# Row maxima and norm scratch in PSUM, operand tiles cleared once, two splits moved to VectorE, in a hybrid decoder layer

## The chip, the core and the metric

The kernel runs on one core of a Trainium2 chip. A core has TensorE for matrix products (PE; its weight loads, which overlap them, are PEld), VectorE (DVE), ScalarE (ACT), GpSimd (POOL), and SyncE (SP), which issues most of the DMAs. Operands lie in SBUF, products are summed in PSUM banks of 128 partitions x 2 KB. The metric is the device time of one execution in microseconds, the median of several runs.

## What is computed

One layer of a decoder on x of 1 x 1024 x 1024 float32. Three token mixers share one input projection: a Mamba-2 state-space mixer (SSD), stick-breaking attention, and native sparse attention (NSA). They are gated, summed and projected. A conv gated MLP with 2816 hidden channels follows; both halves have a norm before and after. The parts of the reference that the change is in, the norm and the selected (`ss`) and window (`sw`) branches of the sparse attention, whose softmax needs the row maxima:

```python
def rms_norm(x, w):
    xf = x.astype(jnp.float32)
    y = xf * lax.rsqrt(jnp.mean(xf * xf, axis=-1, keepdims=True) + NORM_EPS)
    return (y * w.astype(jnp.float32)).astype(x.dtype)

def masked_softmax(s, mask):
    p = jax.nn.softmax(jnp.where(mask, s, NEG), axis=-1)
    return jnp.where(mask, p, 0.0)
...
        ss = (jnp.einsum('bqghd,bgqnkd->bghqnk', qb, ks).astype(jnp.float32) * scale
              - slopes[None, :, :, None, None, None] * dist_s[:, :, None].astype(jnp.float32))
...
        p_sel = masked_softmax(ss, (dist_s >= 0).reshape(bsz, g, 1, NSA_QBLK, n_sel * SEL_BLOCK))
        o_sel = jnp.einsum('bghqm,bgqmd->bqghd', p_sel.astype(vs.dtype),
                           vs.reshape(bsz, g, NSA_QBLK, n_sel * SEL_BLOCK, dh))
...
        sw = (jnp.einsum('bqghd,bkgd->bghqk', qb, kwb).astype(jnp.float32) * scale
              - slopes[:, :, None, None] * dist_w.astype(jnp.float32))
        o_win = jnp.einsum('bghqk,bkgd->bqghd', masked_softmax(sw, wmask).astype(vwb.dtype), vwb)
```

## The kernel before

Work runs feature-major in tiles of 128 x 512. Products are made in a split form: an operand a is written as hi + lo, where hi is a rounded by a copy on ScalarE to a short float32 form, and lo is the rest, a subtraction on DVE or POOL. A product is then three matmuls, hi by hi, hi by lo and lo by hi. So for every weight tile `whi` comes from ACT (L286, L532) and `wlo` from POOL (L291, L533), and many activations have such a pair too. The tile scheduler decides from a modelled timeline which instruction stands where on each engine. In the NSA stage alone PE's instructions are kept in the order of the program (`in_order`).

**The start.** `first_half` reads x, squares it on ACT and adds the squares on DVE (L430, `ss`). `norm` sums `ss` over the partitions by four small products with ones and calls `rsqrt_mean`, which makes the factor 1/sqrt(mean + eps): a logarithm and an exponential on ACT, and one step of refinement on DVE, L254, L256, L257 and L258, with a scratch tile `rv` and the result `rt`, both 128 x 4 in SBUF. ACT spreads `rt` to `rb` (L451), and PE transposes it. There are two calls at the start (two halves of the tokens) and two at the end, in `norm_rows`.

**The NSA stage** (some 420 to 810 us) has 16 steps of 128 queries for one of two groups of heads. For each step `compressed` builds the query operands Q1 and Q2 and does the compressed branch and the top-k choice; `maxima` finds the row maxima of the scores; `attend` makes scores (`ps_s`), exponentials (`wT`), their split (L996 on ACT, L997 on POOL) and the values. The three run interleaved, and PE follows the interleaving as written. `maxima` takes 8 or more banks `ps_t` in turn (two buffers): each is filled by a product and reduced by DVE into `mx` (L959, the tile having been set by POOL, L942). At the end L962 reduces `mx` to `m`, POOL clears the operand tile `MM` (L964), and DVE writes -m, split in two bfloat16 parts, into four columns of it (L966, L967). After `MM_LAG` = 3 further turns of the interleaving PE transposes MM into a bank, and L973 casts that into rows 96 to 128 of Q1. The score products read Q1.

**The MLP** multiplies blocks of weights and activations by a scheme of seven products in place of eight (`weights7`, `product`), so that sums of blocks (`uf`, `uhi`, `ulo`, L532 to L547) are made of each weight, and sums of activations. L1681 and L1682 split the last of these activation sums: for q = 5 on DVE, for q = 4 on POOL, four tiles k = 0 to 3 each. Product 4 (`ahi`, `alo` by these) is among the first that PE does in a weight group, in a bank `psn`; `ahi` has one buffer. Convolutions (L324 on ACT, L328 and L330 on DVE) follow the products.

Of the kernel before, what the change touches and what calls it, by code (L numbers as in the profile page):

```python
# [10 lines left out]
F32 = mybir.dt.float32  # L11
R32 = mybir.dt.float32r
BF = mybir.dt.bfloat16
AF = mybir.ActivationFunctionType
OP = mybir.AluOpType
# [5 lines left out]
DM = 1024  # L21
# [189 lines left out]
def trunk(ctx: ExitStack, tc: tile.TileContext, A: dict, outT: bass.AP, dbg=None):  # L211
    nc = tc.nc
    act = nc.scalar.activation
    V, P = nc.vector, nc.gpsimd
# [35 lines left out]

    def rsqrt_mean(r, v, ps, n):

        act(r, ps, AF.Ln, scale=1.0 / n, bias=eps)
        V.tensor_scalar(v, ps, 1.0 / n, EPS, op0=OP.mult, op1=OP.add)  # L254
        act(r, r, AF.Exp, scale=-0.5)
        V.tensor_tensor(v, v, r, op=OP.mult)  # L256
        V.scalar_tensor_tensor(v, v, -0.5, r, op0=OP.mult, op1=OP.mult)  # L257
        V.scalar_tensor_tensor(r, v, 1.5, r, op0=OP.add, op1=OP.mult)  # L258
# [115 lines left out]
    n1p = n1.enter_context(tc.tile_pool(name="n1", side="right", reuse_waits="tile", bufs=1))  # L374
# [33 lines left out]
    for h in range(2):  # L408
        for k in range(8):
            x = x_t(F32)  # L410
# [31 lines left out]
    def norm(h, ss):  # L442

        ps = ps_d()
        for n in range(4):
            mm(ps[:, n:n + 1], ss[:, n * 128:(n + 1) * 128], ones[:, 0:1], start=True, stop=True)
        rt, v, rq = [n1p.tile([128, 4], F32, name=f"r{n}", bufs=2) for n in "tvq"]
        rsqrt_mean(rt, v, ps[:, 0:4], DM)
        V.tensor_scalar(rq, rt, 0.125, None, op0=OP.mult)
        rb = n1p.tile([128, 4, 128], F32, name="rb")  # L450
        act(rb, rt[:, :, None].to_broadcast([128, 4, 128]), AF.Copy)  # L451
        r = ps_b()
        for n in range(4):
            tr(r[:, n * 128:(n + 1) * 128], rb[:, n, :], ident)
        return rq, r
# [13 lines left out]
    for h, tiles in ((0, [[ps_s, ps_s, ps_t, ps_t]]), (1, [[ps_o, ps_d], [ps_s, ps_s]])):  # L469
        *pss, ss = first_half(h, tiles)  # L470
        rq, r = norm(h, ss)
# [231 lines left out]
def nsa_stage(nc, tc, es, env):  # L703
    E = L(env)
    A, act, V, P, mm, tr, fl = E.A, E.act, E.V, E.P, E.mm, E.tr, E.fl
# [150 lines left out]

    wk = es.enter_context(tc.tile_pool(name="nsa_q", reuse_waits="tile", bufs=2))

    def compressed(g, i):
        qs = wk.tile([128, 256], F32, name="q_in", bufs=3)  # L860
        nc.sync.dma_start(qs, q_d[g, i])
# [9 lines left out]
        ps = pq[:, 256:]  # L871
# [65 lines left out]
    def maxima(g, i):  # L937
# [5 lines left out]
        for h in range(4):  # L943
            for a in range(2):
# [3 lines left out]
                for n, (c0, c1) in enumerate(parts):  # L948
# [9 lines left out]
                        mm(pm[:, w - 128:w], ident_b, mask_d, start=False, stop=True)  # L958
                    V.tensor_reduce(mx[:, h, a, n:n + 1], pm[:, :w], axis=AX, op=OP.max)  # L959
                    yield  # L960
        m = wk.tile([128, 4, 2], F32, name="m")
        V.tensor_reduce(m, mx, axis=AX, op=OP.max)  # L962
        MM = wk.tile([128, 4, 32], BF, name="MM")
        P.memset(MM, 0.0)  # L964
        mv = MM[:, :, 0:4].rearrange("p h (a s) -> p h a s", a=2)
        V.tensor_scalar(mv[:, :, :, 0], m, -1.0, None, op0=OP.mult)  # L966
        V.scalar_tensor_tensor(mv[:, :, :, 1], m, -1.0, mv[:, :, :, 0], op0=OP.mult, op1=OP.subtract)  # L967
        for _ in range(MM_LAG):
            yield
        p3 = ps_tb()  # L970
        for h in range(4):
            tr(p3[96:128, h * 128:(h + 1) * 128], MM[:, h, :], ident_b)
        V.tensor_copy(Q1[96:128, :], p3[96:128])  # L973
# [82 lines left out]
    for n in range(-2, 17):  # L1056
# [3 lines left out]
        if 0 <= n < 16:  # L1060
            g, i = order[n]
# [316 lines left out]
def tail_stage(nc, tc, es, env):  # L1378
# [300 lines left out]
    for q, k, t, place in sorted(parts, key=lambda x: (-x[0], x[1])):  # L1679
        rhs[q][k] = hi, lo = place(), x_t()  # L1680
        act(hi, t, AF.Copy)  # L1681
        (P if q == 4 else V).tensor_tensor(lo, t, fl(hi), op=OP.subtract)  # L1682

    acc = []

# [117 lines left out]
    def norm_rows(ss, W):  # L1803

        n = W // 128
        ps, r = [psn.tile([128, 512], F32, name="psn", tag="psn") for _ in range(2)]
        for m in range(n):
            mm(ps[:, m:m + 1], ss[:, m * 128:(m + 1) * 128], E.ones[:, 0:1], start=True, stop=True)
        rt, v = [fw.tile([128, 4], F32, name=f"r{x}", bufs=2) for x in "tv"]
        E.rsqrt_mean(rt[:, :n], v[:, :n], ps[:, :n], DM)  # L1810
        rb = up_.tile([128, 512], F32, name="u1", bufs=U1_BUFS)
        act(rb[:, :W].rearrange("p (n t) -> p n t", t=128), rt[:, :n, None].to_broadcast([128, n, 128]), AF.Copy)
        for m in range(n):
            tr(r[:, m * 128:(m + 1) * 128], rb[:, m * 128:(m + 1) * 128], E.ident)
        return r
# [81 lines left out]
```

## Time and profile before

| what | value |
|---|---|
| median of 3 runs | 2262.1 us (2256.22 to 2265.59) |
| the profiled execution | 2260.92 us |
| its span | 2259.2 us |
| granted TensorE clock, mean | 0.989 |
| busy: PE, DVE, POOL, ACT | 2177.4, 1329.9, 1275.1, 1205.2 us |
| share of PE in the chain that ended last | 76% |

Times in the trace are microseconds from the start of the span. A row of the timeline gives start, duration, engine, line, operation, output and inputs, and in square brackets the idle time of the engine just before it and what ended that. PE's matmuls overlap, so the spacing of their starts is shorter than their durations. [...]

### The profile page before, as it was taken

The page shows a single profiled execution, that of the slowest core. Times are in us where ns is not written, and L with a number is a line of the kernel's source. Part 1 is how long each engine was busy: PE and PEld are TensorE (multiplying, and loading weights), DVE is VectorE, ACT ScalarE, POOL GpSimd, SP SyncE. Part 2 cuts the span into 40 slices and gives each one's busy share as a digit, 9 for nine tenths or more (in the row PEclk, how much of TensorE's full clock was granted, in tenths as well). Part 3 has the DMA queues.
Part 4 walks back from the last instruction along what each step waited for, and adds up shares of the span by engine and source line. Part 5 has one row for each costly group of instructions (what it writes and reads, how often), then busy time and mean ns, then how long its engine had stood idle before and what let it go on. Part 6 is the DMA issues. An engine that isn't in the chain of part 4 may idle for free.

```text
span 2259.2 us, 30196 instructions
## 1 busy us (share of the span) xinstructions
PE 2177.4 (96%) x10589; PEld 1736.2 (77%) x10589; DVE 1329.9 (59%) x2499; ACT 1205.2 (53%) x2240; POOL 1275.1 (56%) x1120
## 2 busy tenths in 40 slices
PE   7999999998998999999999999999989999989997
PEld 7888889866665678888775678888778888868887
DVE  8665544258557516556536662228945767675776
ACT  7544443466756746676755441236645444466544
POOL 3776741246746634333337656558687777765743
PEclk9999999999999999999999999999999999999999
DMA  4233342321221011212362174235332323255433
GB/s 172 83 112 108 111 143 62 97 84 29 55 75 33 10 59 38 66 57 79 110 214 76 62 242 144 85 126 181 122 98 80 117 94 112 98 173 186 140 100 120
DMA packets 120105, 234.65 MB, mean 104 GB/s; under 512 B 28816, under 2 KB 43088, under 8 KB 119952
## 3 DMA queue, kind: packets, MB, share of 16 engines
q1 hardware_dynamic: 117072, 230.13, 31.1%
q10 hardware_dynamic: 2880, 2.59, 0.3%
q8 instruction: 83, 1.36, 0.3%
q14 instruction: 70, 0.57, 0.1%
HBM read 169.10 MB, written 63.57 MB: 103 GB/s over the span
## 4 chain that ended last, share of the span: by engine, by line
PE 76%; DVE 9%; ACT 5%; POOL 3%; issue 3%; DMA 2%; DVEq 0%; SPq 0%; ACTq 0%; POOLq 0%
PE dense L219 52%; PE ps_s L219 7%; PE ps_o L219 6%; PE ps_t L219 5%; PE ps_b L219 3%; PE psn L219 3%; DVE mx L959 1%; DVE u L328 1%; DMA lo<-m_d 1%; POOL wlo L533 1%; POOL alo L547 0%; ACT h_hi L423 0%; ACT wT L986 0%; POOL wlo L291 0%; DVE yacc L1023 0%
## 5 line engine op out<-in xcount | busy, mean ns | idle before, releaser
L291 POOL TENSOR_TENSOR wlo<-wraw,whi 128x256 fp32r<-128x256 f32 x344 | 273.7, 827 | 265.9 <-ACT whi L286 264.8
L219 PE MATMUL dense<-h_hi,whi 128*128 128x512 f32 x656 | 262.7, 401 | 0.0
L219 PE MATMUL dense<-h_hi,wlo 128*128 128x512 f32 x656 | 256.7, 392 | 0.3 <-POOL wlo L533 0.3
L219 PE MATMUL dense<-h_lo,whi 128*128 128x512 f32 x656 | 256.5, 391 | 0.0
L997 POOL TENSOR_TENSOR wT_lo<-wT,wT_hi 128x512 fp32r<-128x512 f32 x132 | 168.4, 1287 | 95.3 <-ACT wT_hi L996 86.3
L219 PE MATMUL dense<-hi,whi 128*128 128x512 f32 x576 | 214.3, 391 | 1.2 <-ACT whi L286 1.2
L219 PE MATMUL dense<-hi,wlo 128*128 128x512 f32 x512 | 200.7, 393 | 0.5 <-POOL wlo L291 0.4
L219 PE MATMUL dense<-x,uhi 128*128 128x512 f32 x600 | 191.6, 392 | 1.2 <-ACT x L605 1.2
L219 PE MATMUL dense<-lo,whi 128*128 128x512 f32 x448 | 176.1, 394 | 0.0
L286 ACT ACTIVATE whi<-wraw 128x1024 fp32r<-128x1024 f32 (+1 forms) x94 | 92.6, 985 | 152.7 <-PE dense L219 125.7
L542 POOL TENSOR_TENSOR ulo<-uf,uhi 128x1024 fp32r<-128x1024 f32 x38 | 91.8, 2417 | 117.7 <-ACT uhi L541 117.7
L219 PEld LDWEIGHTS dense<-h_hi,wlo 128*128 128x128 f32 x656 | 123.1, 188 | 27.1 <-POOL wlo L533 0.7
L219 PEld LDWEIGHTS dense<-h_hi,whi 128*128 128x128 f32 x656 | 123.7, 189 | 23.6
L219 PEld LDWEIGHTS dense<-h_lo,whi 128*128 128x128 f32 x656 | 123.5, 188 | 22.6
L219 PEld LDWEIGHTS dense<-x,uhi 128*128 128x128 f32 x600 | 113.0, 189 | 26.2 <-ACT x L605 2.4
L1201 POOL TENSOR_TENSOR s_lo<-sa,s_hi 128x512 fp32r<-128x512 f32 (+2 forms) x48 | 53.7, 1120 | 139.5 <-ACT s_hi L1200 139.5
L219 PEld LDWEIGHTS dense<-hi,whi 128*128 128x128 f32 x576 | 108.4, 188 | 25.6 <-ACT whi L286 2.1
L959 DVE TENSOR_REDUCE mx<-ps_t 128x1 f32<-128x384 f32 (+3 forms) x192 | 98.6, 520 | 46.5 <-PE ps_t L219 42.8
L328 DVE SCALAR_TENSOR_TENSOR u<-dense,pv,u 128x511 f32<-128x511 f32 (+1 forms) x140 | 103.4, 741 | 36.9 <-ACT u L324 36.8
L545 POOL TENSOR_TENSOR ulo<-uf,uhi 128x1024 fp32r<-128x1024 f32 x38 | 91.8, 2415 | 41.1 <-ACT uhi L544 39.7
L986 ACT ACTIVATE wT<-ps_s 128x512 f32<-128x512 f32 x132 | 78.4, 594 | 68.2 <-PE ps_s L219 63.8
L219 PEld LDWEIGHTS dense<-hi,wlo 128*128 128x128 f32 x512 | 96.3, 188 | 23.7 <-POOL wlo L291 2.0
(550 smaller groups left out, 6141.8 us busy)
## 6 DMA issues: line engine op xcount, KB each, us to landing
wraw<-in_wfm SPq DMA_DIRECT2D x62, 512.0 KB, 3.7
wraw<-in_wup SPq DMA_DIRECT2D x52, 512.0 KB, 3.6
lo<-m_d SPq DMA_DIRECT2D x58, 256.0 KB, 3.2
g_d<-gate_e SPq DMA_DIRECT2D x48, 256.0 KB, 2.0
s_d<-o SPq DMA_DIRECT2D x48, 256.0 KB, 2.0
ge<-g_d SPq DMA_DIRECT2D x24, 512.0 KB, 3.5
m_d<-u SPq DMA_DIRECT2D x44, 256.0 KB, 2.0
row<-s_d SPq DMA_DIRECT2D x16, 512.0 KB, 4.8
```

Source lines behind the costliest of these rows:

```text
L219: i = f(*a, **k)
L286: act(hi, raw, AF.Copy)
L291: (V if tiles else P).tensor_tensor(lo[:, s], raw[:, s], fl(hi[:, s]), op=OP.subtract)
L328: V.scalar_tensor_tensor(o[:, d:], ps[:, :512 - d], taps[d], o[:, d:], op0=OP.mult, op1=OP.add)
L533: P.tensor_tensor(wlo, raws[0], fl(whi), op=OP.subtract)
L542: P.tensor_tensor(l24, f24, fl(h24), op=OP.subtract)
L545: P.tensor_tensor(l31, f31, fl(h31), op=OP.subtract)
L959: V.tensor_reduce(mx[:, h, a, n:n + 1], pm[:, :w], axis=AX, op=OP.max)
L986: act(w.rearrange("p h q -> p (h q)"), pz, AF.Exp)
L997: P.tensor_tensor(lo, wf, fl(hi), op=OP.subtract)
L1201: (P if SB_SLO else V).tensor_tensor(s_lo[:, c0:], a[:, c0:], fl(s_hi[:, c0:]), op=OP.subtract)
```

## The change

Four edits. In `maxima` the bank for the transposes is taken before the last reduction; the transposes, bfloat16, use its columns 0 to 256, and `m` is now columns 256 to 264 of the same bank. The two MM tiles are made and cleared once, by DVE, ahead of the stage, and used in turn; the 16 clearings on POOL go, and the columns that are never written stay zero. The scratch of `rsqrt_mean` is four columns of the bank in which the sums lie, at all its four calls. Of the q = 4 splits two (k = 2, 3) go from POOL to DVE.

```diff
@@ norm
-        rt, v, rq = [n1p.tile([128, 4], F32, name=f"r{n}", bufs=2) for n in "tvq"]
-        rsqrt_mean(rt, v, ps[:, 0:4], DM)
+        rt, rq = [n1p.tile([128, 4], F32, name=f"r{n}", bufs=2) for n in "tq"]
+        rsqrt_mean(rt, ps[:, 4:8], ps[:, 0:4], DM)
@@ ahead of the NSA stage
     wk = es.enter_context(tc.tile_pool(name="nsa_q", reuse_waits="tile", bufs=2))
+
+
+    MMs = [wk.tile([128, 4, 32], BF, name=f"MM{n}", bufs=1) for n in range(2)]
+    for MM in MMs:
+        V.memset(MM, 0.0)
@@ maxima
-        m = wk.tile([128, 4, 2], F32, name="m")
+
+        pz = ps_t()
+        p3 = pz[:, :256].bitcast(BF)
+        m = pz[:, 256:264].rearrange("p (h a) -> p h a", a=2)
         V.tensor_reduce(m, mx, axis=AX, op=OP.max)
-        MM = wk.tile([128, 4, 32], BF, name="MM")
-        P.memset(MM, 0.0)
+        MM = MMs[i % 2]
         mv = MM[:, :, 0:4].rearrange("p h (a s) -> p h a s", a=2)
         V.tensor_scalar(mv[:, :, :, 0], m, -1.0, None, op0=OP.mult)
         V.scalar_tensor_tensor(mv[:, :, :, 1], m, -1.0, mv[:, :, :, 0], op0=OP.mult, op1=OP.subtract)
         for _ in range(MM_LAG):
             yield
-        p3 = ps_tb()
@@ the last activation sums of the MLP
-        (P if q == 4 else V).tensor_tensor(lo, t, fl(hi), op=OP.subtract)
+        (P if q == 4 and k < 2 else V).tensor_tensor(lo, t, fl(hi), op=OP.subtract)
@@ norm_rows
-        rt, v = [fw.tile([128, 4], F32, name=f"r{x}", bufs=2) for x in "tv"]
-        E.rsqrt_mean(rt[:, :n], v[:, :n], ps[:, :n], DM)
+        rt = fw.tile([128, 4], F32, name="rt", bufs=2)
+        E.rsqrt_mean(rt[:, :n], ps[:, 4:4 + n], ps[:, :n], DM)
```

PE has as many instructions as before, DVE four more, POOL eighteen fewer. Lines behind the edits move (L254 to L258 become L255 to L259, L966, L967 and L973 become L974, L975 and L980), L1682 becomes L1689.

DVE's order around the maxima of the fourteenth step, first before and then in the new kernel (`m` was a tile, and now the output of the reduction is the bank `ps_t`; Q is Q1, `ps_s` holds attention sums):

```order
L959 TENSOR_REDUCE mx<-ps_t 128x1 x2
L934 CAST Q_7556<-ps_b 32x512
L962 TENSOR_REDUCE m<-mx 128x8
L966 TENSOR_SCALAR MM<-m 128x4x2
L967 SCALAR_TENSOR_TENSOR MM<-m,MM 128x4x2
L1020 RECIPROCAL ps_s<-ps_s 128x4
L1021 TENSOR_TENSOR of<-ps_s,sg 128x4
```

```order
L965 TENSOR_REDUCE mx<-ps_t 128x1 x2
L940 CAST Q_7519<-ps_b 32x512
L971 TENSOR_REDUCE ps_t<-mx 128x8
L974 TENSOR_SCALAR MM_3845<-ps_t 128x4x2
L975 SCALAR_TENSOR_TENSOR MM_3845<-ps_t,MM_3845 128x4x2
L1027 RECIPROCAL ps_s<-ps_s 128x4
L1028 TENSOR_TENSOR of<-ps_s,sg 128x4
```

The places are the same and the operands differ; PE's order in the stage is unchanged, and POOL's lacks the clearings.

POOL at the first weight groups of the MLP, before and after (L1682 and L1689 are the split of the activation sums; `wlo`, `alo`, `ulo` are low parts of weights and their sums):

```order
L547 TENSOR_TENSOR alo<-wraw,ahi 128x512
L539 TENSOR_TENSOR uf_15952<-uf_15951,wraw 128x512
L1682 TENSOR_TENSOR x<-x,lo 128x512 x2
L533 TENSOR_TENSOR wlo<-wraw,whi 128x1024
L540 TENSOR_TENSOR uf_15952<-uf_15952,wraw 128x512
L1682 TENSOR_TENSOR x<-x,lo 128x512 x2
L542 TENSOR_TENSOR ulo<-uf_15952,uhi 128x1024
L545 TENSOR_TENSOR ulo<-uf_15951,uhi 128x1024
L533 TENSOR_TENSOR wlo<-wraw,whi 128x1024
L547 TENSOR_TENSOR alo<-wraw,ahi 128x512
```

```order
L548 TENSOR_TENSOR alo<-wraw,ahi 128x512
L540 TENSOR_TENSOR uf_15906<-uf_15905,wraw 128x512
L1689 TENSOR_TENSOR x<-x,lo 128x512 x2
L534 TENSOR_TENSOR wlo<-wraw,whi 128x1024
L541 TENSOR_TENSOR uf_15906<-uf_15906,wraw 128x512
L548 TENSOR_TENSOR alo<-wraw,ahi 128x512
L543 TENSOR_TENSOR ulo<-uf_15906,uhi 128x1024
L546 TENSOR_TENSOR ulo<-uf_15905,uhi 128x1024
L534 TENSOR_TENSOR wlo<-wraw,whi 128x1024
```

The second pair of splits is gone from POOL, and `alo` of the next weight group, with its `ahi` on ACT, stands ahead of the two `ulo`. On DVE the two splits come in here (only after; u and dense are convolution results and product banks):

```order
L331 SCALAR_TENSOR_TENSOR u_15807<-psn,pv,u_15807 128x2
L1689 TENSOR_TENSOR x<-x,lo 128x512
L1588 TENSOR_TENSOR u_15766<-dense,u_15807 128x512
L1643 TENSOR_TENSOR dense<-dense,snap 128x512
L1689 TENSOR_TENSOR x<-x,lo 128x512
L327 COPY psn<-dense 128x2
```

They lie before and behind the two operations on PSUM that stood there alone. PE's twelve products of `psn` now stand together; before, two products with `uhi` stood ahead of the last two of the twelve.

In the state-space stage and around the middle of the down projection the scheduler gives all engines another order of the same instructions.

## Rows read from the trace of the kernel before

**Rows 1.** The page, busy table and costliest groups: busy us, mean ns, idle before.
```profile
PE 2177.4 (96%) x10589; PEld 1736.2 (77%) x10589; DVE 1329.9 (59%) x2499; ACT 1205.2 (53%) x2240; POOL 1275.1 (56%) x1120
...
L219 PE MATMUL dense<-hi,whi 128*128 128x512 f32 x576 | 214.3, 391 | 1.2 <-ACT whi L286 1.2
```

**Rows 2.** What PE waited for: us in total, times, longest.
```profile
PE ps_t L219 <- DVE MM L967: 6.5, 8, 1.4
...
PE ps_s L219 <- ACT dec L1288: 5.5, 4, 2.1
...
PE ps_s L219 <- DVE Q L973: 4.6, 4, 1.7
PE psn L219 <- POOL x L1682: 4.5, 3, 3.8
PE dense L219 <- ACT snap L1550: 4.1, 4, 2.3
```

**Rows 3.** Stretches: length, busy by engine, granted clock, DMA; and one PE row.
```profile
32.30:39.70 7.40, 7.35 (x34) 7.26 (x35) 6.91 (x12) 4.39 (x11) 2.59 (x2) 0.50 0.17 54
1220.00:1230.00 10.00, 10.00 (x42) 5.71 (x42) 2.57 (x8) 5.90 (x16) 8.70 (x8) 0.54 0.32 107
1669.60:1674.50 4.90, 4.86 (x11) 3.80 (x12) 0.00 (x0) 2.37 (x3) 4.90 (x3) 0.50 0.27 101
...
1218.82 0.49 PE L219 MATMUL ps_s<-half,sel 16*128 16x512 f32 x1 [1.29 <-ACT dec L1288]
```

**Rows 4.** Line L1698 of the down projection: duration ns min/median/max, by inputs.
```profile
L1698 DVE TENSOR_TENSOR lo<-psn,hi x39: 673/682/692, 2014.0 to 2162.5; 128x512 fp32r<-128x512 f32 x39
L1698 DVE TENSOR_TENSOR lo<-lo,hi x19: 674/693/2427, 1987.9 to 2188.9; 128x512 fp32r<-128x512 f32 x19
```

**Rows 5.** Lines around the maxima: ns min/median/max; then busy us, mean ns, idle.
```profile
L966 DVE TENSOR_SCALAR MM<-m x16: 177/178/1040, 443.4 to 771.2; 128x8 bf16<-128x8 f32 x16
L967 DVE SCALAR_TENSOR_TENSOR MM<-m,MM x16: 160/178/1239, 443.6 to 771.5; 128x8 bf16<-128x8 f32 x16
L1020 DVE RECIPROCAL ps_s<-ps_s x32: 174/192/192, 469.8 to 810.1; 128x4 f32<-128x4 f32 x32
L883 DVE RECIPROCAL m<-m x16: 167/169/179, 424.9 to 736.6; 128x4 f32<-128x4 f32 x16
...
L967 DVE SCALAR_TENSOR_TENSOR MM<-m,MM 128x8 bf16<-128x8 f32 x16 | 7.2, 453 | 0.4
...
L966 DVE TENSOR_SCALAR MM<-m 128x8 bf16<-128x8 f32 x16 | 5.1, 317 | 1.3
```

**Rows 6.** Timeline of two NSA steps: start, duration, operation, idle before.
```profile
725.85 1.29 POOL L997 TENSOR_TENSOR wT_lo<-wT,wT_hi 128x512 fp32r<-128x512 f32 x1
...
725.99 1.18 DVE L967 SCALAR_TENSOR_TENSOR MM<-m,MM 128x8 bf16<-128x8 f32 x1
...
727.22 0.40 PE L219 MATMUL ps_t<-ident_b,MM 128*32 128x128 bf16 x4 [0.23 <-DVE MM L967]
...
729.36 0.77 PE L219 MATMUL ps_s<-Q,K 128*128 128x512 f32 x1 [1.74 <-DVE Q L973]
...
753.20 0.40 PE L219 MATMUL ps_t<-ident_b,MM 128*32 128x128 bf16 x4 [0.74 <-DVE MM L967]
```

**Rows 7.** Timeline of the first norm.
```profile
29.34 2.30 DVE L258 SCALAR_TENSOR_TENSOR rt<-rv,rt 128x4 f32<-128x4 f32 x1
...
28.75 2.86 POOL L533 TENSOR_TENSOR wlo<-wraw,whi 128x1024 fp32r<-128x1024 f32 x1
...
32.35 1.11 PE L219 MATMUL ps_b<-ident,rb 128*128 128x128 f32 x4 [4.75 <-ACT rb L451]
```

**Rows 8.** Timeline of the first products of the MLP on POOL and PE.
```profile
1662.28 2.53 POOL L1682 TENSOR_TENSOR x<-x,lo 128x512 fp32r<-128x512 f32 x2
1664.77 2.37 POOL L533 TENSOR_TENSOR wlo<-wraw,whi 128x1024 fp32r<-128x1024 f32 x1
...
1668.31 2.52 POOL L1682 TENSOR_TENSOR x<-x,lo 128x512 fp32r<-128x512 f32 x2
...
1669.64 0.79 PE L219 MATMUL psn<-x,ahi 128*128 128x512 f32 x1 [3.81 <-POOL x L1682]
...
1673.65 0.63 PE L219 MATMUL dense<-hi,whi 128*128 128x512 f32 x1
...
1688.45 0.47 PE L219 MATMUL psn<-lo,ahi 128*128 128x512 f32 x1 [1.41 <-DVE u L328]
```

## Prediction

> **What bounds the kernel now.** I read the page's busy table first: TensorE (PE) is busy 2177.4 of 2259.2 us [rows 1]. A change that takes nothing from PE's instruction list can give back only what is left, some 82 us, and the time in which PE runs at the lower of its two clock levels. So I went to PE's waits and asked which of them end on something the change touches. Three do [rows 2]: the transposes of MM wait for L967 on VectorE (DVE), 6.5 us in 8 places; the scores wait for the cast L973 behind those transposes, 4.6 us in 4 places; and the first products of the gated MLP wait for the splits L1682 on GpSimd (POOL), 4.5 us in 3 places, 3.8 of it in one. Two more, `dec` and `snap`, lie where the scheduler puts instructions in a new order, though no code changed there.
>
> Why L967 is late is the second reading. In the down projection an operation of DVE with two SBUF inputs takes 693 ns at the median and up to 2427; the same operation with one input in PSUM never took over 692 ns [rows 4]. L966 and L967 work on 8 columns, read only SBUF and show it too: 178 ns at the median, 1040 and 1239 at most [rows 5]. In the case at 725.99, L967 stands beside POOL and runs until POOL's 1.29 us split of 725.85 is over; the transposes start at 727.22, and the score behind them and behind their cast at 729.36 [rows 6].
>
> **The change part by part.** (1) *Row maxima in PSUM.* After the edit m is written into PSUM, so L966 and L967 have one SBUF input at most. The bank is the one that the transposes took anyway, only three turns earlier, and PE's order in this stage is kept as written, so no new wait for a bank arises. What goes: the 16 L966 spent 5.1 us and the 16 L967 7.2 us where 16 x 0.178 = 2.85 each would do, an excess of 2.2 and 4.4 us [rows 5]. Only what PE waited for counts. I followed the steps in the timeline, and for each took the smaller of PE's gap and the stall. At 727 the gap is 0.23 ahead of the transposes and 1.74 ahead of the score [rows 6]; the 1.00 us by which L967 was late (1.18 - 0.18) passes through the in-order cast to the score, less some slack: 0.9. At 753.20 the gap is 0.74 and all of it goes [rows 6]. Four more steps repeat the pattern, with 0.3, 0.44, 0.85 and 0.15. Sum 3.4 us. The other gaps end on top-k work on DVE and stay.
>
> To this come two small terms. Reading PSUM costs: a reciprocal of 4 columns takes 192 ns from PSUM and 169 from SBUF [rows 5], so 23 ns, twice per step, at the 8 steps where PE waits: +0.4. L966 no longer waits for a clearing on POOL: its idle before is 1.3 us over 16 against 0.4 for L967 [rows 5], 0.06 each, at 8 steps: -0.5. The stage gives **-3.5 us**, between -1.5 (half of the stalls come back on the next operation) and -6 (all 6.6 us of excess).
>
> [...]
>
> (2) *MM cleared once.* 16 clearings leave POOL, and two go to DVE ahead of the stage. POOL is not what PE waits for in this stage, so 0; at worst two DVE operations of the size of L966 delay the first compressed step by 0.4 us.
>
> (3) *Scratch of the norm factor in PSUM.* Four calls. The one that PE waits for is the first: L258 takes 2.30 us instead of 0.16 because it runs into POOL's 2.86 us split of 28.75, and PE's transposes of rb start at 32.35 after 4.75 idle [rows 7]. With rv in PSUM, L256 to L258 pass and rb is there about 2 us sooner. But the next products of PE are sums over ss, whose additions (two SBUF inputs, on DVE) still stand behind that same POOL split. PE then waits there. I take **-0.5**. The ends: 0, and -2.1, which is all that L258 loses (2.30 - 0.16), if the additions pass as well. The other three calls meet no stall on the path: 0.
>
> (4) *Two splits on DVE.* POOL has L1682 at 1662.28 (two of them), then a weight split of 2.37 us, an addition, and only at 1668.31 the last two [rows 8]. PE waits 3.81 us until 1669.64, then runs at the low level: from 1669.6 to 1674.5 the granted clock is 0.50 [rows 3], and a matmul at 1673.65 takes 0.63 us against 0.39 on the mean [rows 1, 8]. In the new order DVE makes the third split right behind the convolution at about 1662.8 and the last behind two PSUM operations. With two SBUF inputs it may wait for POOL's 1664.77 split to end: ready between 1666 and 1667.9 instead of 1669.6. What is late next: the products with `uhi`. Its cast comes on ScalarE after POOL's addition, and now also after the cast `ahi` of the next weights, which has one buffer and waits until PE is through with the twelve psn products. So PE idles again until about 1670.2. I put the first `hi,whi` product at 1672.5 instead of 1673.65: **-1.1** (0 to -2.5). In the next product pair twelve ready matmuls now stand ahead of the psn products that waited 1.41 us at 1688.45 [rows 8]: **-1.4** (0 to -1.4). POOL loses two splits, DVE gains two in a place where it was idle soon after.
>
> (5) *Moved instructions elsewhere.* In the state-space stage all engines get a new order between about 1165 and 1280 us, and in the down projection between 1990 and 2030. No price follows from an order. The first has PE waits for `dec` of 5.5 us and a stretch of 10 us at a granted clock of 0.54 [rows 2, 3]; the second has most of the 4.1 us for `snap` [rows 2]. I take 0 for both and keep both sides: ±5 and ±3. The matmuls of the first gate that moved at the start find PE busy before and after: 0.
>
> Sum: -3.5 - 0.5 - 1.1 - 1.4 = -6.5, on the profiled execution 2260.9 - 6.5 = 2254.4. That execution lies 1.2 us under the median of the runs, 2262.1, so **2255.6 us**, -0.3%.
>
> **The rivals.** *Nothing is won.* Every stall that goes is replaced by one of the next operation with two SBUF inputs, or by ss at the start and `uhi` in the MLP. For it: DVE keeps many such operations, and in (3) and (4) I can name the next one. Against it: in the attention stage the operations behind L967 on the way to PE are a cast from PSUM and PE itself. Time: 2262.
>
> *The clock comes back too.* At the two long idle stretches, 4.75 and 3.81 us [rows 7, 8], PE runs slowly afterwards. From 32.3 to 39.7 the granted clock is 0.50, and from 1669.6 to 1674.5 too [rows 3]. Work that takes 0.63 there and 0.39 else [rows 1, 8] would lose 38% of these 7.4 and 4.9 us, 2.8 and 1.9, if the breaks that remain let the clock stay at its upper level: 2262.1 - 6.5 - 4.7 = 2251. Against it: in both places I still see an idle break of about 2 us.
>
> *Slower, by the new order of the state-space stage.* That stage is where PE waits and loses its clock together: the 10 us at 0.54 follow on the `dec` wait of 1.29 us that ends at 1218.82, and 4.6 of them would be saved at 1.00 [rows 3]; the longest such wait is 2.1 us [rows 2]. One more wait of that kind with a slow stretch behind it costs up to 6.7 us, which cancels the gain; two cost 13.4 and make 2269. So it decides from the second on. For it: there are four `dec` waits in the stage, and only one of them has such a stretch behind it so far. Against it: the new order may as well remove that one.
>
> *The edits do not free DVE.* If an operation with a PSUM input stalls when its output or second input in SBUF meets POOL, L966 and L967 stay as long as they are; that is the first rival's time, 2262, with other rows to show it. [Rows 4] speak against it: 39 such operations, none over 692 ns.
>
> **How the numbers follow.** Forecast 2255.6: 0.48. Nothing won or not freed, 2262: 0.24. Clock back too, 2251: 0.17. Slower stage, 2269: 0.11. The unknown terms of (1) to (5), which hardly all fall on one side, reach from about 2248 to 2264 around the forecast, and the runs before scatter from 2256.2 to 2265.6. I take 2246 to 2267, which leaves out the slower case and the far end of the clock case. Half a percent is 11.3 us, about what a measurement of this kernel can tell from no change: under 2250.8 is faster, over 2273.4 slower. Faster: half of the clock case and a part of the forecast's good end, 0.22. Slower: the state-space case with three stretches, and what no row here shows, 0.07. Within: 0.71.
>
> **What would show it.** Right: L966 and L967 at about 200 ns at most, PE's waits for MM near 2 us in sum instead of 6.5, no wait of PE for POOL's x of over 1 us, and the first `hi,whi` product of the MLP one us sooner against the product before the gap. Wrong: L967 still above 1 us beside POOL; the wait for rb replaced by one of the same end for ss (then (3) is 0); a DVE split over 2 us with PE behind it; or a granted clock under 0.6 in more than one 10 us window between 1160 and 1280, or in none.

## The result and the profile after

The changed kernel takes 2248.85 us (median of 6 runs, 2244.07 to 2253.81) against 2263.2 (6 runs, 2256.22 to 2265.59): a ratio of 0.9944, 95% interval 0.9929 to 0.9959, or -14 us. Forecast were 2255.6 and -6.5 us. The direction is right and the time lies in the range; the size is a good half of it short. By the prediction's own line for "faster", 2250.8 us, to which it gave 0.22, the median lies just on the faster side.

The page of the changed kernel, busy table (as in [rows 1]), and what PE waited for (as in [rows 2]: us in total, times, longest us):

```profile
PE 2170.4 (97%) x10589; PEld 1732.6 (77%) x10589; DVE 1322.8 (59%) x2503; ACT 1203.3 (54%) x2240; POOL 1269.1 (57%) x1102
...
PE ps_s L219 <- ACT dec L1295: 4.3, 5, 2.1
PE ps_t L219 <- DVE MM L975: 3.2, 4, 1.0
PE ps_b L219 <- ACT rb L452: 2.9, 1, 2.9
PE ps_s L219 <- DVE Q L980: 2.8, 3, 1.3
...
PE dense L219 <- DVE ss L431: 1.8, 1, 1.8
...
PE psn L219 <- DVE x L1689: 1.7, 1, 1.7
PE dense L219 <- ACT uhi L542: 1.5, 1, 1.5
...
PE ps_s L219 <- ACT wT_hi L1003: 1.2, 1, 1.2
```

The wait for MM halves (6.5 to 3.2), and the one for POOL's split of 3.8 us is gone. That for Q seems to fall from 4.6 to 2.8, but 1.2 us of the difference is one gap of the score products (1.24 us both times) that the profile of the changed kernel puts down to `wT_hi`, the last line: the four places together went from 4.6 to 4.1. Three waits took a place: `ss` at the start, and `x` and `uhi` in the MLP.

To see where the time went I set instructions of the two traces against each other one by one and took the shift at the borders of the stages. Two sums explain most of it: PE's waits in the stage, and what the lower clock costs (clock loss), as the sum over the stretches of length x (1 - granted clock). The granted clock (PEclk) is the mean of a stretch as a share of full speed; in both traces it stands at one of two levels, 1.00 or 0.50. All in us:

| stage (times of before) | shorter by | PE's waits | clock loss | forecast |
|---|---|---|---|---|
| start, 0 to 330 | 0.2 | 15.5 to 15.6 | 5.1 to 3.4 | 0.5 |
| sparse attention, 500 to 815 | 6.3 | 21.8 to 17.2 | 3.4 to 1.7 | 3.5 |
| state space, 1150 to 1290 | 4.6 | 9.4 to 7.7 | 6.8 to 5.1 | 0 |
| first products of the MLP, 1640 to 1760 | 0.7 | 6.5 to 6.1 | 3.4 to 1.7 | 2.5 |
| down projection, 1980 to 2060 | 1.2 | 5.7 to 5.2 | 1.7 to 1.7 | 0 |
| whole span | 12.9 | 68.4 to 62.4 | 24.3 to 18.3 | 6.5 |

PE's waits fell by 6.0 us, almost the forecast in sum, though not stage by stage. The other half is clock that the kernel no longer loses, 6.0 us, for which the forecast had nothing. (At the start the regained 1.7 us do not show in the time; why, this trace does not tell.)

In the attention stage the stalls are gone. The lines of the maxima of the changed kernel (ns min/median/max, as in [rows 5]):

```profile
L974 DVE TENSOR_SCALAR MM<-ps_t x16: 159/176/179, 443.4 to 764.9; 128x8 bf16<-128x8 f32 x16
L975 DVE SCALAR_TENSOR_TENSOR MM<-ps_t,MM x16: 160/176/178, 443.6 to 765.1; 128x8 bf16<-128x8 f32 x16
```

At most 179 ns, where 1040 and 1239 stood; and with an input in PSUM they take what they took from SBUF, 176 against 178. The fourteenth step, the one of [rows 6], in the timeline of PE (start, duration, idle before in brackets):

```profile
723.87 0.40 PE L219 MATMUL ps_t<-ident_b,MM 128*32 128x128 bf16 x4
725.52 0.71 PE L219 MATMUL ps_s<-Q,K 128*128 128x512 f32 x2 [1.25 <-DVE Q L980]
...
726.92 0.39 PE L219 MATMUL ps_o<-wT_lo,V_hi 128*65 128x512 f32 x1
```

The gap ahead of the transposes is gone and that ahead of the score went from 1.74 to 1.25 us. The third line is a surprise: 0.39 us, where the same matmul of before took 0.63. The stretches behind this gap, of before and then of the changed kernel (length, busy PE, PEld, DVE, ACT, POOL, granted clock, DMA share, GB/s):

```profile
729.30:733.00 3.70, 3.64 (x11) 2.43 (x12) 0.56 (x1) 1.39 (x3) 1.38 (x2) 0.55 0.00 0
```

```profile
725.50:729.20 3.70, 3.68 (x21) 2.75 (x22) 1.78 (x4) 2.39 (x5) 2.50 (x2) 1.00 0.00 0
...
565.00:568.00 3.00, 3.00 (x11) 1.99 (x10) 0.92 (x3) 1.65 (x3) 0.63 (x1) 0.52 0.20 46
```

Before, PE did 11 pieces of work at 0.55 there, now 21 at 1.00. The last line shows the reverse at another place: the changed kernel ran three microseconds at 0.52 where before did not. Such stretches are what moves the clock column of the table.

At the start (as in [rows 7]) POOL, DVE and PE of the changed kernel read:

```profile
28.78 2.79 POOL L534 TENSOR_TENSOR wlo<-wraw,whi 128x1024 fp32r<-128x1024 f32 x1
```

```profile
29.29 0.15 DVE L259 SCALAR_TENSOR_TENSOR rt<-dense,rt 128x4 f32<-128x4 f32 x1
29.47 2.65 DVE L431 TENSOR_TENSOR ss<-ss,sq 128x512 f32<-128x512 f32 x1
```

```profile
30.60 0.66 PE L219 MATMUL ps_b<-ident,rb 128*128 128x128 f32 x4 [2.88 <-ACT rb L452]
33.06 1.84 PE L219 MATMUL dense<-ones,ss 128*128 128x1 f32 x8 [1.81 <-DVE ss L431]
```

The last factor operation takes 0.15 us in place of 2.30, and the next addition of squares, which reads only SBUF, takes 2.65. PE waits 2.88 and 1.81 where it waited 4.75.

In the MLP (as in [rows 8]), DVE, POOL and PE:

```profile
1652.70 1.76 DVE L1689 TENSOR_TENSOR x<-x,lo 128x512 fp32r<-128x512 f32 x1 [0.86 <-POOL x L1689]
...
1655.58 1.66 DVE L1689 TENSOR_TENSOR x<-x,lo 128x512 fp32r<-128x512 f32 x1
```

```profile
1653.86 2.83 POOL L534 TENSOR_TENSOR wlo<-wraw,whi 128x1024 fp32r<-128x1024 f32 x1
1656.65 1.73 POOL L541 TENSOR_TENSOR uf<-uf,wraw 128x512 f32<-128x512 f32 x1
```

```profile
1652.72 0.50 PE L219 MATMUL psn<-x,ahi 128*128 128x512 f32 x1 [0.43 <-POOL x L1689]
...
1657.30 0.50 PE L219 MATMUL psn<-x,ahi 128*128 128x512 f32 x1 [1.68 <-DVE x L1689]
...
1659.53 0.73 PE L219 MATMUL dense<-x,uhi 128*128 128x512 f32 x2 [1.50 <-ACT uhi L542]
...
1661.49 0.63 PE L219 MATMUL dense<-hi,whi 128*128 128x512 f32 x1
```

Each split takes about 1.7 us beside POOL, and POOL's own operations there grow from 2.37 and 1.27 us to 2.83 and 1.73, so `uf` comes later. The cast `uhi` on ACT stands behind `uf` and also behind the cast `ahi`, which waits for PE's products of `psn`:

```profile
1657.88 0.63 ACT L547 ACTIVATE ahi<-wraw 128x512 fp32r<-128x512 f32 x1 [1.40 <-PE psn L219]
1658.42 1.06 ACT L542 ACTIVATE uhi<-uf 128x1024 fp32r<-128x1024 f32 x1
```

`uf` is ready at 1658.38 (1656.65 + 1.73), and `uhi` starts at 1658.42, as `ahi` ends: both hold it equally long here. PE's wait of 3.81 us became one of 1.68 and one of 1.50.

### The profile page after: what moved, and what is told of

It is laid out like the page before. It is cut to its first block, busy times and chain, and to the rows that moved or that the text cites. A ratio compares the mean times of both kernels' runs of the same rounds, so it can differ in the third digit from the quotient of the medians.

```text
span 2246.3 us, 30163 instructions
## 1 busy us (share of the span) xinstructions
PE 2170.4 (97%) x10589; PEld 1732.6 (77%) x10589; DVE 1322.8 (59%) x2503; ACT 1203.3 (54%) x2240; POOL 1269.1 (57%) x1102
## 4 chain that ended last, share of the span: by engine, by line
PE 79%; DVE 8%; ACT 5%; issue 3%; POOL 3%; DMA 2%; SPq 0%; DVEq 0%; ACTq 0%; POOLq 0%
PE dense L219 55%; PE ps_s L219 7%; PE ps_o L219 6%; PE ps_t L219 5%; PE ps_b L219 4%; PE psn L219 3%; DVE mx L965 1%; DVE u L329 1%; ACT wT L993 0%; ACT h_hi L424 0%; ACT wT_hi L1003 0%; DMA lo<-m_d 0%; POOL wlo L534 0%; POOL alo L548 0%; DVE x L1523 0%
## 5 line engine op out<-in xcount | busy, mean ns | idle before, releaser
L292 POOL TENSOR_TENSOR wlo<-wraw,whi 128x256 fp32r<-128x256 f32 x344 | 273.4, 825 | 271.9 <-ACT whi L287 270.8
L546 POOL TENSOR_TENSOR ulo<-uf,uhi 128x1024 fp32r<-128x1024 f32 x38 | 91.7, 2413 | 38.8 <-ACT uhi L545 36.8
```

The costliest lines, as they stand in the source:

```text
L292: (V if tiles else P).tensor_tensor(lo[:, s], raw[:, s], fl(hi[:, s]), op=OP.subtract)
L546: P.tensor_tensor(l31, f31, fl(h31), op=OP.subtract)
```

## The experiments

My theory was that three independent parts act: the maxima (operations of DVE that read only SBUF are stretched beside POOL's, as L966 and L967 to 1.04 and 1.24 us at most from 0.18), the scratch at the start (which moves only a wait, but also gives the state-space stage another order), and the splits. The rivals: that POOL's clearing, not this stretching, held the attention stage; that the state-space gain is scatter; that the splits are worth their forecast.

**m in PSUM alone.**

```diff
-        m = wk.tile([128, 4, 2], F32, name="m")
+        pz = ps_t()
+        p3 = pz[:, :256].bitcast(BF)
+        m = pz[:, 256:264].rearrange("p (h a) -> p h a", a=2)
```

(the later `p3 = ps_tb()` is gone, POOL still clears MM)

> The kernel before with one edit: m lies in the bank of the transposes; POOL still clears MM at each step, and the order on every engine is that of before. Theory A (L966 and L967 were late because they read SBUF only and stood beside a POOL operation): both at most 0.18 us, PE's waits for MM 6.5 to about 3.2 us and for Q 4.6 to about 2.8, and the end of the stage earlier by 5 to 6.5 us, of which some 4 are waits and the rest the clock; the run about 2255. Theory B (they were late, or PE was, because POOL's clearing waits for PE's transposes, 8.1 us, with the splits of wT queued behind it): the stage gains under 1.5 us.

Measured: 2255.8 us in one run, before 2263.3 beside it; attention stage 5.4 us shorter than in the trace of before. Lines of the maxima, what PE and what POOL waited for in the stage:

```profile
L968 DVE TENSOR_SCALAR MM<-ps_t x16: 176/177/179, 444.7 to 767.1; 128x8 bf16<-128x8 f32 x16
L969 DVE SCALAR_TENSOR_TENSOR MM<-ps_t,MM x16: 160/176/179, 444.9 to 767.3; 128x8 bf16<-128x8 f32 x16
```

```profile
PE ps_s L219 <- DVE Q L974: 4.1, 4, 1.2
PE ps_t L219 <- DVE MM L969: 3.7, 5, 1.1
```

```profile
POOL MM L966 <- PE ps_t L219: 7.2, 7, 3.1
```

The stalls go with m in PSUM although POOL still waits 7.2 us to clear MM. That is theory A. (Q at 4.1 and not 2.8 is no contradiction: here the profile puts all four gaps down to Q.)

**MM cleared once, m in SBUF.**

```diff
+    MMs = [wk.tile([128, 4, 32], BF, name=f"MM{n}", bufs=1) for n in range(2)]
+    for MM in MMs:
+        V.memset(MM, 0.0)
...
-        MM = wk.tile([128, 4, 32], BF, name="MM")
-        P.memset(MM, 0.0)
+        MM = MMs[i % 2]
```

> The kernel before with the other half of that edit: two MM tiles cleared once by DVE, m stays in SBUF; PE, ACT and SP in the order of before. Theory A: L966 and L967 still take up to 1.0 to 1.2 us somewhere; PE's waits for MM stay above 5 us; the stage ends 0 to 1.5 us earlier. Theory B: the stage ends 4 to 6 us earlier and POOL no longer waits 8.1 us.

Measured: 2260.4 us in one run; the stage is 2.6 us shorter than in the trace of before, more than theory A allowed. Lines of the maxima and PE's wait:

```profile
L968 DVE TENSOR_SCALAR MM<-m x16: 166/178/1084, 443.7 to 768.9; 128x8 bf16<-128x8 f32 x16
L969 DVE SCALAR_TENSOR_TENSOR MM<-m,MM x16: 167/178/1255, 443.9 to 769.2; 128x8 bf16<-128x8 f32 x16
```

```profile
PE ps_t L219 <- DVE MM L969: 6.0, 7, 1.9
```

The stalls stay, so the clearing is not their cause. PE's waits in the stage are 20.6 us against 21.8, and the clock loss is 1.7 against 3.4: the clearing is worth about 1 us of waits, more than the forecast had for it, and the rest of this kernel's gain is 1.7 us of clock.

**The scratch at the start alone.**

```diff
-        rt, v, rq = [n1p.tile([128, 4], F32, name=f"r{n}", bufs=2) for n in "tvq"]
-        rsqrt_mean(rt, v, ps[:, 0:4], DM)
+        rt, rq = [n1p.tile([128, 4], F32, name=f"r{n}", bufs=2) for n in "tq"]
+        rsqrt_mean(rt, ps[:, 4:8], ps[:, 0:4], DM)
```

> The kernel before with the scratch of the norm factor in PSUM at the two calls of the start alone. The order in the state-space stage is then that of the changed kernel on all engines, although no line of that stage was touched. Theory A (the 4.7 us that the changed kernel wins between 1160 and 1280 us come from the order that the scheduler chose): that stage 4 to 5 us shorter, the start 0 (the wait for rb 2.9 instead of 4.7, and a new one for ss of 1.8), the attention stage 0, the down projection 0 to 1.5; about 2255. Theory B (they come from the earlier start of the stage after the attention, against DMAs that keep their time): the stage as before, about 2260.

Measured: 2262.0 us in one run. The state-space stage, in the new order, is 0.5 us shorter than before, not 4 to 5; and the attention stage, in which nothing differs from before, is 2.8 us longer. PE's waits in the state-space stage are 7.1 us, as in the changed kernel, but the clock loss is 10.3 instead of 5.1. So one trace against one trace doesn't settle a stage to better than some 3 us. That called for timed runs of the parts.

**The splits alone**, in one run and then timed.

```diff
-        (P if q == 4 else V).tensor_tensor(lo, t, fl(hi), op=OP.subtract)
+        (P if q == 4 and k < 2 else V).tensor_tensor(lo, t, fl(hi), op=OP.subtract)
```

> The kernel before with the two splits on VectorE alone. The state-space stage keeps the order of before, the down projection has a new one. Theory A (what the splits give back is taken by the next wait, uhi, and by POOL operations that grow from 2.4 to 2.8 us beside them): the third split 1.7 us long, PE's longest wait for a split 1.7 instead of 3.8, a new one for uhi of 1.5, gain there 0.5 to 1 us, nothing between 1160 and 1280; about 2259. Theory B (the splits are worth 2.5 us and the new order around took it): gain at the first product of the MLP 2 us or more.

> The kernel before with the two splits on VectorE alone, timed. By the look at it the first products of the MLP gain under 1 us and the down projection, in its new order, 1 to 3. Theory A (the splits are worth what the first products gain, the rest is scatter): ratio 0.999 to 1.000. Theory B (the new order of the down projection is a gain that repeats): ratio 0.9975 to 0.999.

Measured: 2258.0 us in the one run; timed (12 runs), a ratio of 0.9994, interval 0.9983 to 1.0005: nothing that can be told from zero. In both traces the MLP's first products gain 0.2 and 0.7 us, and the down projection, in its new order, 2.7 both times. The ratio lies in theory A's range. But its interval reaches down to 0.9983, into theory B's, so that a gain of up to 3.8 us, and with it the 2.7 that both traces show, is not excluded.

**The maxima alone, and the scratch alone, timed; the changed kernel again.** The edits are those of the first two experiments together, of the third with the same in `norm_rows`, and all.

> The kernel before with the whole edit of the maxima (m in the bank of the transposes, two MM tiles cleared once) and nothing else; PE, ACT and SP in the order of before throughout. Theory A (the edit is most of the change): attention stage 5 to 7 us shorter than in a kernel without it, no stall of L966 or L967, ratio 0.9965 to 0.998. Theory B (the 6.3 us seen in the changed kernel's one trace were half of them the clock of that one execution): ratio 0.998 to 0.9995.

> The kernel before with the scratch of the norm factor in PSUM at all four calls, and nothing else; the order in the state-space stage is that of the changed kernel. Theory A (that order is worth 4.7 us): ratio 0.997 to 0.9985. Theory B (state-space stages differ by two or three us between executions of one order, and the edit does nothing at the start): ratio 0.9985 to 1.001.

> The changed kernel once more, for a second trace of it beside the parts, on one chip: ratio 0.993 to 0.996. If the three parts are independent, their ratios multiply to this one. Theory A expects the attention stage 5 to 7 us shorter again and the state-space stage 4 to 5; theory B expects the attention stage the same and the state-space stage 0 to 3.

Measured: maxima 0.9962 (0.9946 to 0.9979; 12 runs), scratch 0.998 (0.9966 to 0.9994; 12 runs), all 0.9936 (0.9917 to 0.9955; 6 runs). With the splits' 0.9994 the three parts multiply to 0.9936; with intervals this wide that agrees with independent parts but does not prove them. The maxima are worth about 9 us (5 to 12), somewhat more than their theory A. The scratch with its order is worth 4 to 5 by its median ratio, but the interval, 1 to 8 us, reaches into theory B, and the traces don't show where so much would come from: with the scratch at all calls the span is 2.3 us shorter than before, with that at the start alone 1.1 longer, and the state-space stage is 0.7 and 0.5 shorter, not 4.7.

The traces of all these kernels, with those of the four experiments below, give each stage several times. Attention stage, 500 to 815 us (us; clock loss as above):

| kernel | length | PE's waits | clock loss |
|---|---|---|---|
| before; scratch at the start; splits; scratch; splits again | 315.0, 317.8, 316.3, 315.2, 317.8 | 21.8, 22.8, 23.0, 21.7, 22.9 | 3.4, 5.1, 3.4, 3.4, 5.1 |
| MM cleared once | 312.4 | 20.6 | 1.7 |
| m in PSUM | 309.6 | 18.2 | 1.7 |
| changed; maxima; changed again; start pieces; two pieces; no split | 308.7, 307.1, 307.2, 310.2, 308.7, 307.2 | 17.2, 17.1, 17.2, 17.0, 17.1, 17.2 | 1.7, 0, 0, 3.4, 1.7, 0 |

Waits are the same within 1.3 us for one code, and fall by 5.3 on the mean. The clock loss comes in steps near 1.7 us; it differs between executions of one code by as much as two of them, and falls from 4.1 to 1.1 on the mean. The slow stretch near 528, behind gaps of 0.87 and 0.79 us before, stands in all five traces of the first line and in one of the six of the last, where the first of the two gaps is 0.58; the one behind the gap of [rows 6], between 729 and 737, stands in three of the five and in none of the six. The state-space stage:

| order | length | PE's waits | clock loss |
|---|---|---|---|
| of before: before, m in PSUM, MM, splits, maxima, splits again | 140.0, 138.9, 142.1, 138.3, 137.7, 138.7 | 9.4, 8.3, 7.2, 9.0, 9.8, 9.5 | 6.8, 6.9, 11.9, 5.1, 3.4, 5.1 |
| new: scratch at the start, scratch | 139.5, 139.3 | 7.1, 6.8 | 10.3, 10.2 |
| new, with the maxima: changed, changed again, start pieces, two pieces, no split | 135.4, 134.4, 135.6, 135.7, 134.0 | 7.7, 6.5, 7.8, 7.9, 7.9 | 5.1, 5.1, 5.1, 5.1, 3.4 |

The new order costs PE 7.4 us of waits against 8.9 on the mean: 1.5 us come from the order. The clock loss does not follow it: with the scratch alone it is 10 both times, with the maxima as well 5 or less each time. Why an edit that lies 350 us earlier should matter there, or whether these seven are chance, the runs don't settle.

**The top-k scores in PSUM**, on top of the change, to see whether other operations are freed in the same way.

```diff
-            im = wk.tile([128, 16], F32, name="im")
+            im = pq[:, 0:16]
```

> The changed kernel, and in the compressed branch the 16 block scores of the top-k choice, im, lie in the query's own bank (columns 0 to 16) instead of SBUF. In the changed kernel the three additions and products on im take 0.53, 0.73 and 0.77 us on the mean for 16 columns. Theory A (any small operation of VectorE that reads only SBUF is stretched beside POOL, and one PSUM input frees it): all three at 0.16 to 0.20 us; PE's waits for MM 3.2 to about 2.3 us, since one of the four ends on such an operation ahead of L975; the attention stage 0.5 to 2 us shorter. Theory B (they are long for another reason, the mask that they read): as long as before, no gain. The order of the state-space stage moves too, which is worth up to 2 us of waits there in the other direction.

Measured: 2275.6 us (7 runs), ratio 1.0065 (1.0047 to 1.0083): slower than before, and some 27 us slower than the changed kernel. Groups of DVE in the attention stage of the changed kernel, then of this one (busy us, mean ns | idle):

```profile
L904 DVE TENSOR_TENSOR im<-im,fa 128x16 f32<-128x16 f32 x8 | 6.2, 771 | 0.0
```

```profile
L904 DVE TENSOR_TENSOR ps_b<-ps_b,fa 128x16 f32<-128x16 f32 x8 | 1.4, 174 | 0.0
```

and what PE waited for:

```profile
PE ps_b L219 <- DVE left L909: 18.6, 8, 3.1
...
PE ps_t L219 <- DVE MM L975: 2.2, 3, 1.0
```

The operations do what theory A says, all three at 0.17 us (L903 and L909 had 0.73 and 0.56), and the wait for MM falls to 2.2. But `ps_b` is a pool of one bank. As long as `im` lives in it, PE can't have it for the next transposes: 18.6 us of a wait that was not there, with a clock loss in the stage of 13.6 us behind it. This was a mistake in my expectation, which looked at the operations and not at who else needs the bank. The change itself has no such price, since its bank is the one that the transposes use next.

**POOL's first weight split in four pieces**, on top of the change; the order stays that of the changed kernel on all engines.

```diff
-        P.tensor_tensor(wlo, raws[0], fl(whi), op=OP.subtract)
+        for c in range(0, 2 * n, 256 if turn[0] == 2 else 2 * n):
+            e = c + (256 if turn[0] == 2 else 2 * n)
+            P.tensor_tensor(wlo[:, c:e], raws[0][:, c:e], fl(whi[:, c:e]), op=OP.subtract)
```

> The changed kernel, and POOL's first split of a 128x1024 weight (2.8 us) is four splits of 128x256; the order on all engines is that of the changed kernel. Theory A (the additions of the squares, and behind them PE's wait for ss of 1.8 us, stand behind that one operation): the longest addition 2.65 to about 1.1 us, the wait for ss 1.8 to 0.3 to 0.8, the products of the second norm 1.0 to 1.5 us earlier, and up to 2 us more if PE's slow stretch behind it gets shorter. Theory B (POOL gives way to VectorE no sooner between its operations, or the squares on ScalarE are late): the wait stays at 1.5 us or more.

Measured: ratio 0.9918 (0.9898 to 0.9938), 2244.55 us (4 runs). Timeline of DVE, POOL and PE:

```profile
29.34 1.03 DVE L431 TENSOR_TENSOR ss<-ss,sq 128x512 f32<-128x512 f32 x1
```

```profile
28.65 4.19 POOL L536 TENSOR_TENSOR wlo<-wraw,whi 128x256 fp32r<-128x256 f32 x4
```

```profile
30.47 1.11 PE L219 MATMUL ps_b<-ident,rb 128*128 128x128 f32 x4 [2.92 <-ACT rb L452]
31.71 1.84 PE L219 MATMUL dense<-ones,ss 128*128 128x1 f32 x8
```

The addition takes 1.03 us where it took 2.65, and the wait for `ss` shrinks from 1.81 to 0.13. The products behind start at 31.71 instead of 33.06. So it was that one operation of POOL; theory A. The gain at the start is about 1 us against the changed kernel's trace; the lower median is within the scatter of the others.

**A second weight split in pieces**, the one beside the fourth split of the MLP.

```diff
-        P.tensor_tensor(wlo, raws[0], fl(whi), op=OP.subtract)
+        step = {2: 256, 28: 512}.get(turn[0], 2 * n)
+        for c in range(0, 2 * n, step):
+            P.tensor_tensor(wlo[:, c:c + step], raws[0][:, c:c + step], fl(whi[:, c:c + step]), op=OP.subtract)
```

> The kernel with the first weight split of POOL in four pieces, and besides the weight split that stands beside the fourth activation split of the MLP (2.83 us on POOL in the changed kernel) in two halves; the order on all engines is that of the changed kernel. Theory A (in the MLP uhi is what is late, and the splits no longer matter): the fourth split ends 0.5 to 1.3 us sooner and PE's wait for it falls from 1.7 to 0.4 to 1.2 us, but the wait for uhi grows by as much, and the first product hi,whi is not earlier by over 0.3 us. Theory B (PE's chain there goes through the split): it is 0.5 to 1.3 us earlier. Ratio in both 0.991 to 0.994, as far as the first four pieces repeat.

Measured: ratio 0.9937 (0.9925 to 0.995), 2247.99 us (5 runs). Timeline of PE:

```profile
1656.62 0.50 PE L219 MATMUL psn<-x,ahi 128*128 128x512 f32 x1 [0.69 <-DVE x L1691]
...
1660.06 2.17 PE L219 MATMUL dense<-x,uhi 128*128 128x512 f32 x4 [2.71 <-ACT uhi L544]
1662.03 0.63 PE L219 MATMUL dense<-hi,whi 128*128 128x512 f32 x1
```

The wait for the split falls from 1.68 to 0.69 us, that for `uhi` grows from 1.50 to 2.71. From PE's first wait in this place to the product hi,whi it is 9.00 us (1653.03 to 1662.03), against 8.77 in the changed kernel (1652.72 to 1661.49). POOL and ACT show why it is no sooner:

```profile
1654.18 3.52 POOL L536 TENSOR_TENSOR wlo<-wraw,whi 128x512 fp32r<-128x512 f32 x2
```

```profile
1658.95 1.06 ACT L544 ACTIVATE uhi<-uf 128x1024 fp32r<-128x1024 f32 x1 [1.12 <-POOL uf L543]
```

`ahi` now comes early and `uhi` waits for POOL's `uf` alone, which is later, as the two halves take POOL 3.52 us where the whole took 2.83. So the last split is not what sets the end here, theory A; but the edit delays `uf` as well, and what the split alone would give is not measured.

**The change without the splits.** The edit is the one of the splits, undone.

> The changed kernel with the two activation splits back on POOL. Theory A (the splits are worth nothing by themselves, as their own run says, 0.9994): ratio 0.993 to 0.9955, like the changed kernel; the down projection 2 us longer in its other order, the first products of the MLP 1 to 2 us shorter in theirs. Theory B (the splits give 2 us or more): 0.9955 to 0.997.

Measured: ratio 0.9939 (0.9919 to 0.996), 2245.29 us (5 runs): the same as with them. Theory A. Its timeline of PE in the MLP shows why:

```profile
1650.69 0.50 PE L219 MATMUL psn<-x,ahi 128*128 128x512 f32 x1 [0.43 <-POOL x L1685]
...
1660.71 0.63 PE L219 MATMUL dense<-hi,whi 128*128 128x512 f32 x1
...
1674.89 0.47 PE L219 MATMUL psn<-lo,ahi 128*128 128x512 f32 x1 [0.28 <-DVE u L328]
```

The product hi,whi comes 10.02 us after the first wait, as before, where the changed kernel needs 8.77. But the wait of 1.41 us in the next product pair [rows 8] is down to 0.28 without the splits, as also in the two traces of the scratch alone (0.28 and 0.27), and the changed kernel waits 1.49 us there, for `snap`. What the splits win at the first pair, 1.25 us, they lose at the second, 1.21. The down projection of this kernel is 2.1 us shorter than before, not longer than in the changed kernel as I expected, so the order of that stage is not the splits' doing alone. Which of its pieces matters stays open.

No version here stands clear of the changed kernel: the ratios of the three that are as fast, 0.9918, 0.9937 and 0.9939, have intervals that overlap with its 0.9944 and 0.9936.

## Why the prediction was right in direction and short in size

(1) *Maxima: -3.5 forecast.* The mechanism is right: m in PSUM removes the stalls, by itself and beside the same POOL work. PE's waits fell by 4.6 us in the pair of traces, 5.3 on the mean of the stages, against 3.5. Gap by gap the six terms 0.9, 0.74, 0.3, 0.44, 0.85 and 0.15 came out as 0.71, 0.74, 0.29, 0.44, 1.41 and 0.14. The one that was mis-sized is the step at 679, whose gap went whole:

```profile
679.25 0.40 PE L219 MATMUL ps_t<-ident_b,MM 128*32 128x128 bf16 x4 [1.41 <-DVE MM L967]
```

A gap of 0.44 us behind `oT` on ACT, at 583, went too, which I had not counted. The term for PSUM reads, +0.4, is zero: 176 ns against 178 for these operations of 8 columns. The 23 ns between the two reciprocals, from which I took it, were too high for them. What the working left out is the clock: it took a stall for its length, while a gap could be followed by a slow stretch worth 1.7 us more (3.4 us at 0.50). 3.0 us of the 8.2 by which the stage is shorter on the mean are this. It was visible in the trace of before: the matmuls behind the gap of [rows 6] run at 0.55.

(2) *Clearing once: 0 forecast, and 0.5 in (1) for the wait of L966.* About 1 us of PE's waits, by the kernel with m in PSUM alone against those with both (18.2 against 17.1): a gap of 0.30 us that was left at 679 and one of 0.40 at 582 go only with the clearing. The step that said that POOL keeps nobody waiting in this stage was wrong by the other half us.

(3) *Scratch: -0.5 forecast.* Nearly right, and as worked out: PE's wait for `rb` is 1.87 us shorter and `ss` took its place with 1.81. The products of `ss` start 0.2 us sooner (33.06 instead of 33.26), which is near the prediction's own sign that (3) is 0. That the additions stand behind POOL's one long split is shown by the pieces: 1.03 us for 2.65. What the timed runs give for the scratch, 4 to 5 us, is not won here, and stays without a cause.

(4) *Splits: -2.5 forecast.* The first part was right in its place: the product hi,whi came 1.25 us earlier against the first wait (8.77 instead of 10.02 us), forecast 1.1, with `uhi` late next. It repeats: 8.76 to 8.78 in the five other traces with the splits on DVE and POOL's weight split there in one piece, and 9.4 to 10.02 in the seven without the splits. The second part, -1.4 from the products that now stand ahead of the waiting ones, failed. The changed kernel waits in that place too, on another thing, as its timeline of PE shows:

```profile
1676.85 0.50 PE L219 MATMUL dense<-hi,uhi 128*128 128x512 f32 x1 [1.49 <-ACT snap L1557]
```

I had covered the late products with ready ones and not asked whether their bank had been read out (`snap`). And without the splits the new order leaves only 0.28 us in this place, so that they lose there what they win before. Over the stage 0.7 us are left in this trace, no more than what kernels without the splits show there (0.7 with the maxima alone, 1.9 and 2.9 with the scratch alone), and by the timed runs the splits are worth nothing that can be told from zero.

(5) *Moved instructions: 0, ±5 and ±3 forecast.* Both came out on the good side, 4.6 and 1.2 us in the pair of traces. Of the first, 1.5 us are the order's by the mean of the traces; the rest is clock that varies.

*The sum.* That PE's waits fell by 6.0 us where 6.5 were forecast is luck in part: the attention stage gave 1.1 more than its term, the state-space stage 1.7 where 0 stood, and the first products of the MLP 0.4 of 2.5. And half a percent was too wide for what a measurement can tell: the interval of the ratio reaches 0.15% to either side.

*The rivals.* "The clock comes back too" had the right time, 2251, for reasons that were half right. I named the two longest waits, and in the pair of traces 1.7 us of clock did come back at each of them, but slow stretches remained there (at the start until 38.8 instead of 39.7), and over all traces the MLP loses 2.4 us of clock on the mean with the splits and without. What repeats is the clock behind the gaps near 528 and 729 in the attention stage, of 0.79 to 1.74 us in the trace of before: slow in five and three of the five traces without an edit of the maxima, and in one and none of the six with both. "Slower by the new order" didn't occur; its price, a wait and a slow stretch together, is real, as the kernel with `im` in PSUM shows on another stage. "Not freed" is refuted by the lines at 179 ns, and "nothing is won" by the ratio.

*The signs.* The wait for MM is 3.2 us and not near 2. Of the signs of being wrong one more came true beside that of `ss`: no stretch of 10 us between 1160 and 1280 lies under a granted clock of 0.6 (the lowest, from 1226.7, has 0.66). That is one execution's chance: the second trace of the changed kernel has one of 0.50, from 1215.1.

## What to carry to other kernels

Small operations of VectorE that read only SBUF took up to seven times their length here (1.24 us for 0.18) beside a POOL operation, and one PSUM operand freed them (179 ns at most) at little cost in their own time: L966 and L967 took 176 ns for 178, and the top-k lines L901, L906 and L908, which moved to PSUM without having been stretched, 8 or 9 ns more (L906: 173 for 165); but ask who needs the bank next, since holding the only one of a pool cost 18.6 us of waits. When a wait is removed, count also what PE's clock did behind it, which here doubled the gain (6.0 us of waits, 6.0 of clock). And give each stage several traces before its gain is ascribed to an edit: in the attention stage the waits of one code repeated within 1.3 us, while its clock loss differed by up to 3.4.

## What the runs showed of the hardware

- PE's clock loss in a stage comes in steps of about 1.7 us in this kernel (0, 1.7, 3.4, 5.1 in the attention stage). Over a whole span it is 15.5 to 19.4 us in the six traces with the whole edit of the maxima (the kernel with `im` in PSUM aside) and 20.2 to 25.8 in the seven without it; executions of one code differ by up to two steps of 1.7 us in the attention stage.
- The contention goes both ways: beside DVE's splits POOL's 128x1024 split takes 2.83 us instead of 2.37, and four pieces of 128x256 beside the additions 4.19 us where one whole took 2.79 (a 128x256 split of POOL takes 0.74 us at the median in the changed kernel, L292).
